# A softmax kernel in a hardware loop of three chunks: each load issued as two transfers of 32 KB per partition instead of one of 64 KB

## The chip, the cores and the metric

One core of one Trainium2 chip. The metric is the device time of one execution in microseconds (us); several executions are timed and their median is quoted. Ratios are the mean time of one kernel's fast runs over that of the other's of the same rounds, so they are not quite the ratio of the medians quoted beside them.

## The reference

A softmax over the last axis of a float32 tensor of 16 x 256 x 32768, with a temperature of 1.0.

```python
def reference(logits, temperature):
    scaled = logits / temperature
    scaled = scaled - scaled.max(axis=-1, keepdims=True)
    exp_scaled = np.exp(scaled)
    return (exp_scaled / exp_scaled.sum(axis=-1, keepdims=True)).astype(np.float32)
```

537 MB are read and 537 MB written, each once.

## The kernel before

Each of the 4096 rows is cut in two, which makes 64 chunks of 128 partitions x 16384 numbers (64 KB per partition, 8.39 MB). A chunk stays in one of three buffers: it is loaded, reduced and exponentiated in four pieces on VectorE and ScalarE, the two halves of a row are combined, the chunk is scaled in place and stored. All transfers are issued by the sync engine, into one queue.

```python
    def step(i: int, turn=None, per_turn: int = 0) -> None:
        g, c = divmod(i, C)
        end = turn is None and g == G - 1
        store(i, _END_DMA if end else CW, turn, per_turn)
        j = i + _BUFS - 1
        if i and j < n_chunks:
            end = turn is None and j // C == G - 1
            load(j, _END_DMA if end else CW, turn, per_turn)
        if c == C - 1 and g + 1 < G:
            ...    # cut: normalise the next chunk

    per_turn = 3
    first = per_turn
    turns = (n_chunks - (_BUFS - 1) - C - first) // per_turn     # 19
    ...    # cut: the first loads, the first chunk
        for i in range(first):
            step(i)
        with tc.For_i(0, turns, 1, iteration_sync="reg_based") as turn:
            for i in range(first, first + per_turn):
                step(i, turn, per_turn)
        for i in range(first + turns * per_turn, n_chunks):
            step(i)
```

Step i stores chunk i and loads chunk i+2 into the buffer that chunk i-1 has left. One turn of the hardware loop has three steps, one for each buffer. The framework puts in all waits: it hands out eight DMA semaphores in turn (counters that a transfer raises when it has landed, and that instructions wait for), and it starts anew with the first of them inside the loop.

Of the kernel before, what the change touches and what calls it, by code (L numbers as in the profile page):

```python
# [9 lines left out]
_CW = 16384  # L10
_BUFS = 3
_PIECE = 4096
_END_DMA = 4096
_END_PIECE = 4096
_DVE_SHARE = 0.625
# [4 lines left out]
def kernel(  # L20
# [19 lines left out]
    CW = min(_CW, W)  # L40
    C = W // CW
# [21 lines left out]
    def spans(total: int, step: int) -> list[tuple[int, int]]:  # L63
        return [(s, min(step, total - s)) for s in range(0, total, step)]

    def rows(i: int, turn, per_turn: int):
        g = i // C
        if turn is None:
            return slice(g * P, (g + 1) * P)
        return bass.ds(turn * (per_turn // C * P) + g * P, P)  # L70

    def load(i: int, step: int, turn=None, per_turn: int = 0) -> None:
        c = i % C
        for s, n in spans(CW, step):
            nc.sync.dma_start(
                out=buf[i % _BUFS][:, s : s + n],
                in_=x[rows(i, turn, per_turn), c * CW + s : c * CW + s + n],
            )

    def store(i: int, step: int, turn=None, per_turn: int = 0) -> None:  # L80
        c = i % C
        for s, n in spans(CW, step):
            nc.sync.dma_start(  # L83
                out=o[rows(i, turn, per_turn), c * CW + s : c * CW + s + n],
                in_=buf[i % _BUFS][:, s : s + n],
            )
# [70 lines left out]
# [4 lines that stand above are left out]
        j = i + _BUFS - 1  # L161
        if i and j < n_chunks:
            end = turn is None and j // C == G - 1
            load(j, _END_DMA if end else CW, turn, per_turn)
        if c == C - 1 and g + 1 < G:
            end = turn is None and g + 1 == G - 1
            normalise(g + 1, _END_PIECE if end else _PIECE)

    per_turn = 3
# [3 lines left out]

    with tc.manual_schedule():
        for i in range(_BUFS):
            load(i, _END_DMA if i < C else CW)
        normalise(0, _PIECE)
        for i in range(first):
            step(i)
# [5 lines that stand above are left out]
# [35 lines left out]
```

## Time and profile before

| | before |
|---|---|
| timed with the changed kernel | 2498.11 us median (2490.05 to 2508.91, 4 runs) |
| profiled span | 2489.5 us |
| DMA queue busy | 99.9% of the span, 431 GB/s |
| VectorE, ScalarE busy | 63%, 55% |

One more view: the waits of the sync engine, which issues all transfers. The columns are: who waited on which line for what, the total in us, how often, and the longest.

```profile
SPq L83 <- DVE x L150: 2102.8, 66, 40.2
SPq L83 <- DMA x<-in_logits_dram: 168.1, 19, 9.5
```

Line 83 is the store. It waits for the engines to finish a chunk. 19 times, once a turn, it also waits for a load, at most 9.5 us; that is a wait which is passed on the way, with the one for VectorE behind it.

### The profile page before, as it was taken

The numbers are of one execution on the slowest core, as the hardware profiler recorded it, in microseconds if no ns is written. First come the engines' busy times: TensorE is split into PE (matmuls) and PEld (weight loads), VectorE is DVE, ScalarE is ACT, GpSimd is POOL, SyncE is SP. The second block draws the span as 40 slices with busy tenths as digits, with TensorE's granted clock in tenths as the row PEclk, the third lists the DMA queues.
The fourth block names the chain that finished last, engine by engine and source line by source line (L and its number), as shares of the span: only waits on it lengthen the run. The fifth ranks groups of instructions, "written<-read, shape, count | busy, mean of one in ns | idle before, by whom it ended". The sixth has DMA issues, their size and how long they took to land. (4 is left out here: it accounts for less than half of the span.)

```text
span 2489.5 us, 4388 instructions
## 1 busy us (share of the span) xinstructions
DVE 1579.6 (63%) x1216; ACT 1368.7 (55%) x833; POOL 0.2 (0%) x4
## 2 busy tenths in 40 slices
DVE  6575665766657666576566665766657666576565
ACT  5464554646546455464554655646546455464555
POOL 0000000000000000000000000000000000000000
DMA  9999999999999999999999999999999999999999
GB/s 421 421 438 433 426 433 435 425 437 437 431 433 435 435 433 436 432 435 432 438 431 436 433 436 437 430 436 433 437 428 437 433 438 429 436 433 432 426 405 404
DMA packets 19733, 1073.79 MB, mean 431 GB/s; under 512 B 2192, under 2 KB 2192, under 8 KB 2192
## 3 DMA queue, kind: packets, MB, share of 16 engines
q1 hardware_dynamic: 19728, 1073.75, 99.9%
q14 instruction: 5, 0.04, 0.0%
HBM read 536.87 MB, written 536.87 MB: 431 GB/s over the span
## 5 line engine op out<-in xcount | busy, mean ns | idle before, releaser
L115 DVE TENSOR_REDUCE nm<-x 128x1 f32<-128x4096 f32 x256 | 1113.7, 4412 | 646.6 <-DMA x<-in_logits_dram 635.9
L122 ACT ACTIVATE x<-x,nm 128x4096 f32<-128x4096 f32 x256 | 949.2, 3708 | 1017.3 <-DVE nm L115 1002.2
L153 ACT ACTIVATE x<-x,f 128x1536 f32<-128x1536 f32 x256 | 382.3, 1564 | 73.5 <-DVE f L147 73.5
L150 DVE TENSOR_SCALAR x<-x,f 128x2560 f32<-128x2560 f32 x256 | 380.2, 1548 | 2.3
L135 DVE CUSTOM_DVE_ANT_0 ttj<-ee,ssum 128x4 f32<-128x4 f32 x64 | 10.4, 163 | 222.5 <-ACT ee L132 222.5
L122 ACT ACTIVATION_READ_ACCUMULATOR x<-x,nm 128x1 f32 x256 | 47.7, 186 | 0.0
L132 ACT ACTIVATE ee<-nm,nMh 128x4 f32<-128x4 f32 x64 | 18.0, 282 | 0.0
L147 DVE TENSOR_SCALAR f<-ee,rS 128x4 f32<-128x4 f32 x64 | 14.7, 229 | 2.2
L146 DVE RECIPROCAL rS<-Sh 128x1 f32<-128x1 f32 x64 | 10.5, 164 | 2.2
L94 DVE TENSOR_TENSOR nMh<-nMh 128x1 f32<-128x1 f32 x64 | 10.2, 159 | 2.2
L94 DVE TENSOR_TENSOR Sh<-Sh 128x1 f32<-128x1 f32 x64 | 10.2, 159 | 2.2
L130 DVE TENSOR_REDUCE nMh<-nm 128x1 f32<-128x4 f32 x64 | 10.0, 157 | 2.2
L91 DVE STREAM_SHUFFLE Sh<-Sh 128x1 f32<-128x1 f32 x64 | 9.7, 152 | 0.0
L91 DVE STREAM_SHUFFLE nMh<-nMh 128x1 f32<-128x1 f32 x64 | 9.7, 151 | 0.0
L122 ACT ACT_TABLE_LOAD x1 | 1.3, 1283 | 8.1 <-DMA x<-in_logits_dram 8.1
L135 DVE DVE_READ_ACCUMULATOR2_ANT Sh<- 128x1 f32 x64 | 5.3, 82 | 0.0
L91 DVE LOAD_MASK_SELECT nMh<-nMh x64 | 0.9, 14 | 2.8
L91 DVE LOAD_MASK_SELECT Sh<-Sh x64 | 0.9, 14 | 2.8
L201 POOL MEMSET const-bfloat16-1.0<- 128x1 bf16 x1 | 0.1, 103 | 0.0
L201 POOL MEMSET const-uint8-127<- 128x1 uint8 x1 | 0.1, 102 | 0.0
L201 POOL MEMSET const-float32-0.0<- 128x1 f32 x1 | 0.1, 99 | 0.2 <-issue 0.2
L201 POOL MEMSET const-float32-1.0<- 128x1 f32 x1 | 0.1, 99 | 0.0
## 6 DMA issues: line engine op xcount, KB each, us to landing
x<-in_logits_dram SPq DMA_DIRECT2D x8, 2048.0 KB, 29.3
out_dram<-x SPq DMA_DIRECT2D x4, 2048.0 KB, 15.9
out_dram<-x SPq DMA_DIRECT2D x63, 29.3
x<-in_logits_dram SPq DMA_DIRECT2D x62, 48.0
```

Source lines behind the costliest of these rows:

```text
L91: nc.vector.stream_shuffle(out=v[:, j + 1 : j + 2], in_=v[:, j : j + 1], mask=mask)
L94: nc.vector.tensor_tensor(out=v[:, j + 1 : j + 2], in0=v[:, j : j + 1], in1=v[:, j + 1 : j + 2], op=op,)
L115: nc.vector.tensor_reduce(out=nm[:, k : k + 1], in_=xc, axis=X, op=A.max, negate=True)
L122: nc.scalar.activation(out=xc, in_=xc, func=Exp, bias=nm[:, k : k + 1], scale=inv_t, accum_out=ssum[:, k : k + 1],)
L130: nc.vector.tensor_reduce(out=nMh[:, 0:1], in_=nm, axis=X, op=A.min)
L132: nc.scalar.activation(out=ee, in_=nm, func=Exp, bias=nMh[:, n_rounds : n_rounds + 1], scale=-1.0)
L135: nc.vector.tensor_tensor_reduce(out=ttj, in0=ee, in1=ssum, scale=1.0, scalar=0.0, op0=A.mult, op1=A.add, accum_out=Sh[:, 0:1],)
L146: nc.vector.reciprocal(out=rS, in_=Sh[:, n_rounds : n_rounds + 1])
L147: nc.vector.tensor_scalar_mul(out=f, in0=ee, scalar1=rS)
L150: nc.vector.tensor_scalar_mul(out=xc[:, :cut], in0=xc[:, :cut], scalar1=f[:, k : k + 1])
L153: nc.scalar.activation(out=xc[:, cut:], in_=xc[:, cut:], func=Copy, scale=f[:, k : k + 1])
L201: nc = _bacc.Bacc("TRN2", target_bir_lowering=False, num_devices=1)
```

## The change

The intent: when a chunk's load comes in two halves, VectorE can start on the first half while the second is on its way, so that the store is ready earlier. The end of the kernel, with transfers of 16 KB per partition, stays as it is.

```diff
+_LOAD = 8192
...
-            load(j, _END_DMA if end else CW, turn, per_turn)
+            load(j, _END_DMA if end else _LOAD, turn, per_turn)
...
-            load(i, _END_DMA if i < C else CW)
+            load(i, _END_DMA if i < C else _LOAD)
```

The program that is built from it differs where the diff doesn't show it. These are the waits of the first store in the loop, before and after (abridged, with the growth of the awaited count in brackets; semaphores named `own` are those of the loop):

```
before: DMACopy out_0_dram<-x0_58 [waits DMAHW0_own (16 more each turn), DVE_own, DMAHW2_own, Activation_own, DMAHW3_own, DMAHW4_own, ...]
after:  DMACopy out_0_dram<-x0_58 [waits DMAHW0_own (32 more each turn), DVE_own, DMAHW3_own, Activation_own, DMAHW4_own, DMAHW5_own, DMAHW6_own, ...]
```

## The prediction

> **What bounds the kernel now.** I read the page first (busy shares, slices, queues), then the sync engine's timeline in the middle and at the loop's end, then times to landing, and last the built program's waits.
>
> ```profile
> DVE 1579.6 (63%) x1216; ACT 1368.7 (55%) x833; POOL 0.2 (0%) x4
> DMA  9999999999999999999999999999999999999999
> q1 hardware_dynamic: 19728, 1073.75, 99.9%
> HBM read 536.87 MB, written 536.87 MB: 431 GB/s over the span
> ```
>
> The engines are a third idle or more; the one DMA queue is busy for 99.9% of the 2489.5 us span. In the DMA view of 200 to 2200 us it moves 434 GB/s, so a transfer of 128 rows of 64 KB (8.39 MB) takes 8.39/434 = 19.3 us, and a chunk (one load, one store) 38.7. 64 chunks at 38.7 are 2477 us: nearly the whole span. A steady chunk in the timeline:
>
> ```profile
> 1042.79 0.34 SPq L83 DMA_DIRECT2D out_dram<-x  x1
> 1043.34 0.35 SPq L75 DMA_DIRECT2D x<-in_logits_dram  x1
> 1052.98 17.40 DVE L115 TENSOR_REDUCE nm<-x 128x1 f32<-128x4096 f32 x4 [10.32 <-DMA x<-in_logits_dram]
> 1075.49 5.94 DVE L150 TENSOR_SCALAR x<-x,f 128x2560 f32<-128x2560 f32 x4
> 1075.55 5.97 ACT L153 ACTIVATE x<-x,f 128x1536 f32<-128x1536 f32 x4 [1.15 <-DVE f L147]
> 1081.78 0.34 SPq L83 DMA_DIRECT2D out_dram<-x  x1
> ...
> out_dram<-x SPq DMA_DIRECT2D x63, 29.3
> x<-in_logits_dram SPq DMA_DIRECT2D x62, 48.0
> ```
>
> A store lands 29.3 us after its issue, though it needs only 19.3: at issue some 10 us of the next chunk's load are still ahead of it. VectorE's wait (10.32) is for that same load. So each store enters the queue 10 us before it would run dry, and the queue never does. It does run dry once, where the hardware loop ends, because the sync engine there waits for every transfer of the loop:
>
> ```profile
> 2319.10 0.35 SPq L75 DMA_DIRECT2D x<-in_logits_dram  x1
> 2367.91 0.34 SPq L83 DMA_DIRECT2D out_dram<-x  x1
> 2368.30 0.42 SPq L75 DMA_DIRECT2D x<-in_logits_dram  x1
> ...
> DMA to landing us min/median/max: 48.1/48.1/48.1
> ...
> DMA to landing us min/median/max: 42.4/42.4/42.4
> ```
>
> The two landing lines belong to the two loads shown. The first lands at 2319.10 + 48.1 = 2367.2, only then is the store issued (2367.91), and the load behind it lands at 2368.30 + 42.4 = 2410.7. Between the two landings lie one store and one load, 38.7 us of work, but 43.5 pass. **One drain of the queue costs 4.8 us**, of which 0.7 is the barrier between 2367.2 and 2367.91. This is the number that my prediction rests on.
>
> **What the Trainium skill says.** Four places of its page "DMA: Bandwidth & Descriptors". "Where 436 GB/s comes from" gives 435 GB/s as the ceiling of the core's 16 DMA engines; the trace agrees with 434 in the steady part, so a faster steady state isn't to be had. "Queues, rings and completion order" says each engine takes descriptors in ring order, which agrees with the landings: 48.0 for a load is 10 of the load before, 19.3 of the store, 19.3 of its own. "Anatomy of one DMA" gives about 2 us of fixed cost (for the GpSimd path), mostly completion[...]. Here the first load's 2 MB (4.8 us at 434 GB/s) are issued at 0.74 and VectorE starts on them at 8.10: 2.5 us. "Why a DMA increments its semaphore by 16 and not by 1" says that two DMAs in flight on one semaphore can't be told apart by its count and each slot should have its own. No trace of before shows it, but the compiler of this kernel must respect it, and there the change hurts.
>
> **The change part by part.**
>
> *Added transfers.* 62 loads become 124: 62 x 128 = 7,936 more data packets, 62 x 16 = 992 more small ones. From the DMA view: 200 to 2200 us (64 KB packets alone) has 14,881 packets, 1,648 of them small, at 100.2%: 1.002 x 16 x 2000 / 13,233 = 2.423 us per packet. 2472 to 2484 us (16 KB packets) has 367, 48 small, at 101.7%: 1.017 x 16 x 12 / 319 = 0.612. Four of those are 2.448, so three more packets cost 25 ns, 8 each. Each engine gets 62 x 8 = 496 more: about 4 us, with completions **5 us**. Issuing costs the sync engine 62 x 0.35 us, beside a full queue: nothing.
>
> *Earlier start.* The first half of a chunk lands 9.7 us before the second, so VectorE does two of four reductions (2 x 4.35 = 8.7 us) earlier and the store is ready 8.7 us earlier. With a full queue this makes the queue longer, 18.7 us for 10, and nothing faster. At the end of the kernel too: the last loads and stores follow one another in the queue, and the stretch from 2396 to 2489 is 98% busy.
>
> *A new wait.* The program has eight DMA semaphores, handed out in turn, and inside the loop the counting starts anew. Before, a turn has six transfers (store, load, three times), each with its own semaphore. Now it has nine: store, load a, load b, three times; the ninth, load b of the third step, gets the first semaphore, that of the turn's first store. In the built program this first store waits for that semaphore to reach 32 more per turn (16 before), that is for **both** transfers of the turn before on it, and the second is the transfer issued immediately ahead of this store. So the store, the first of every turn, can't enter the queue until the queue is empty. The data doesn't need it: that load goes to another buffer. The order of instructions alone doesn't show it; the list of waits does.
>
> How often: (64 - 2 - 1 - 3) // 3 = 19 turns; the first has no turn before it, so **18 drains**; the one at loop exit is there already. Is the wait really last? Yes: the store's chunk is finished some 18 us before that load lands (the longer queue), and even on the old schedule 10 us before. After a drain the turn's other stores are issued with 18 us or more queued, and nothing else runs dry: the second store also needs the first landed, at about 22 us, while the load behind the first runs till 41.
>
> Cost of one: 4.8 as above, less the barrier's 0.7, plus about 0.2 to get from the landing to the issue: 4.3 us. It contains completion, issue, first data, and a slowdown when all engines restart together (the load after the restart took 2410.7 - (2367.91 + 21.7) = 21.1 us after its store landed, 21.7 being that store's own time to landing, where 19.3 is usual). A turn has four more transfers after those two; at the kernel's start, likewise from rest, such transfers lose some tenths each, so I take **4.7**. 18 x 4.7 = 85 us, with 5 for packets **+90 us**: the profiled span becomes about 2580. The three timed runs of before average 2502, so 2502 + 90 = 2592; I shade it to **2588**, because 4.7 rests on one drain.
>
> **The rivals.**
> 1. *Saturated, nothing happens* (no drain, only packets): 2505 + 5 = 2510. For it: 99.9% busy. Against it: the wait's count, which is in the program.
> 2. *The earlier start pays at the end.* The chain that ended last goes through the load that lands at 2410.7 and then VectorE; 8.7 us less there would give 2496. Against it: the queue is busy behind that chain until the end.
> 3. *Drains are cheap*: only landing to issue and issue to data, 2 us, because the restart slowdown at the loop's end was chance. 18 x 2 + 5 = 41: 2543, within 2%.
> 4. *Half rows read worse from HBM.* The 16 KB windows show 1% per byte for the smaller pieces; twice that on half of the bytes were 25 us on top of the drains.
>
> **Range and chances.** Low end: 2.6 us a drain, 47 + 5 on 2496 (between the fastest run and the mean): 2548. High end: 5.9 a drain, 106 + 5 on 2509: 2620. 2% of 2505 is 50 us, so 2.5 us a drain passes it; rivals 1 and 3 together get 0.12. Faster needs more than the 435 ceiling has: 0.01. Slower: 0.87.
>
> **What would show it right or wrong.** In the changed profile: 18 stores, 116.3 + 4.7 = 121 us apart, issued right after the landing of a load with VectorE long idle, and a sync wait on a load that ends them; queue share near 97%, mean rate near 1073.8/2580 = 416 GB/s; 28,661 packets (19,733 + 7,936 + 992); stores landing at a median of about 38 us (29.3 + 8.7), those right after a drain at 22; VectorE's busy time unchanged. If the page still shows 431 GB/s and no such gaps, rival 1 is right and I misread the wait. If the gaps are there but 2 us each, rival 3. A rate below 428 GB/s between drains would be rival 4.

## The result

The changed kernel takes 2567.07 us (median of 4, 2565.23 to 2568.25), the kernel before 2498.11. The ratio is 1.0273 with a 95% interval of 1.0224 to 1.0322: slower. The time lies within the predicted range, 21 us under its point.

The page of the changed kernel: span, queue, totals, and the transfers with their median time from issue to landing.

```profile
span 2563.4 us, 4789 instructions
...
DVE 1585.3 (62%) x1216; ACT 1368.7 (53%) x833; POOL 0.2 (0%) x4
...
DMA  9999999999999999999999999999999999999999
...
DMA packets 28660, 1073.79 MB, mean 419 GB/s; under 512 B 3184, under 2 KB 3184, under 8 KB 3184
...
q1 hardware_dynamic: 28656, 1073.75, 98.4%
...
x<-in_logits_dram SPq DMA_DIRECT2D x124, 4096.0 KB, 47.4
...
out_dram<-x SPq DMA_DIRECT2D x63, 38.3
```

The bytes and the engines' work are those of before; the rate has fallen from 431 to 419 GB/s, and the queue is no longer busy all the time. The "9" in all 40 slices doesn't show that, since a slice of 64 us hides a gap of 3. A store now takes 38.3 us to land where it took 29.3: the queue ahead of it is 9 us longer. So the earlier start works as intended. It just doesn't help.

One turn of the loop in the timeline of the changed kernel (start, duration, engine, line; the last bracket is idle time before it, and what ended it):

```profile
973.72 5.94 DVE L151 TENSOR_SCALAR x<-x,f 128x2560 f32<-128x2560 f32 x4
...
998.60 8.75 DVE L116 TENSOR_REDUCE nm<-x 128x1 f32<-128x4096 f32 x2 [0.96 <-DMA x<-in_logits_dram]
998.87 0.36 SPq L84 DMA_DIRECT2D out_dram<-x  x1
999.50 1.58 SPq L76 DMA_DIRECT2D x<-in_logits_dram  x2
...
1020.84 0.36 SPq L84 DMA_DIRECT2D out_dram<-x  x1
1021.41 0.88 SPq L76 DMA_DIRECT2D x<-in_logits_dram  x2
...
1061.14 0.36 SPq L84 DMA_DIRECT2D out_dram<-x  x1
1061.81 0.90 SPq L76 DMA_DIRECT2D x<-in_logits_dram  x2
...
1119.08 0.35 SPq L84 DMA_DIRECT2D out_dram<-x  x1
```

VectorE's part of the chunk is scaled at 973.72 + 5.94 = 979.7. Its store is issued at 998.87, 19.2 us later, and 0.3 us after VectorE was woken by another chunk's load (998.60). From this store to the next of its kind, at 1119.08, a turn takes 120.2 us; before, it took 116.0, three chunks of 38.66 (from the load issued at 1004.92 to that at 2280.63 are 33 chunks, 1275.7 us). And in the waits of the sync engine:

```profile
SPq L84 <- DMA x<-in_logits_dram: 1351.9, 38, 55.6
SPq L84 <- DVE x L151: 892.8, 48, 37.1
```

The store's waits for a load have risen from 168.1 us (at most 9.5) to 1351.9 (at most 55.6), and from 19 to 38 times. They are of two kinds: from 998 to 1062 us, about half a turn, the same view has two, 74.2 us together, the longer of 55.6. The shorter one, before the turn's third store, is passed on the way as before. The long one, before the first, is new, and it ends last. It happens 18 times: the drained stores are issued from 277.11 to 2321.61 us, 120.3 us apart on average, each about 0.4 us after the landing.

**Where one drain's time goes**, from the times to landing of these same transfers (a drain: the queue runs empty before the next transfer is issued). In order: the two halves of the load ahead, the store, the first and the second half behind it, the turn's last two halves.

```profile
DMA to landing us min/median/max: 47.3/51.9/56.4
...
DMA to landing us min/median/max: 21.8/21.8/21.8
...
DMA to landing us min/median/max: 30.9/30.9/30.9
...
DMA to landing us min/median/max: 41.1/41.1/41.1
...
DMA to landing us min/median/max: 47.2/51.7/56.3
```

The load issued second at about 942.1 lands 56.4 us later, at 998.5. The store issued at 998.87 lands after 21.8, at 1020.7: 22.2 us after the load, where one transfer takes 19.3 in a full queue, so 2.9 are lost. The two halves behind it land at 999.5 + 30.9 and 1000.1 + 41.1 = 1041.2: 20.5 us for the pair where 19.4 are usual, 1.1 lost. From there to the landing of the last load of the turn (issued at 1062.4, 56.3 to landing, so 1118.7) 77.5 us pass for four transfers of 19.3 or 19.4: nothing lost. Together 4.0 us in this turn.

### The profile page after: what moved, and what is told of

It reads as the page before. It is cut to its first block, busy times and chain, and to the rows that moved or that the text cites. A ratio compares the mean times of both kernels' runs of the same rounds, so it can differ in the third digit from the quotient of the medians.

```text
span 2563.4 us, 4789 instructions
## 1 busy us (share of the span) xinstructions
DVE 1585.3 (62%) x1216; ACT 1368.7 (53%) x833; POOL 0.2 (0%) x4
## 3 DMA queue, kind: packets, MB, share of 16 engines
q1 hardware_dynamic: 28656, 1073.75, 98.4%
## 5 line engine op out<-in xcount | busy, mean ns | idle before, releaser
L136 DVE CUSTOM_DVE_ANT_0 ttj<-ee,ssum 128x4 f32<-128x4 f32 x64 | 10.4, 162 | 222.5 <-ACT ee L133 222.5
## 6 DMA issues: line engine op xcount, KB each, us to landing
out_dram<-x SPq DMA_DIRECT2D x63, 38.3
```

What stands on the lines that cost most here:

```text
L136: nc.vector.tensor_tensor_reduce(out=ttj, in0=ee, in1=ssum, scale=1.0, scalar=0.0, op0=A.mult, op1=A.add, accum_out=Sh[:, 0:1],)
```

## The experiments

The theory: nine transfers a turn, eight semaphores, so the first store of a turn waits for the transfer issued just ahead of it and the queue runs dry once a turn. The main rival: halved loads are slow in themselves (more packets, a worse order of reads, upset timing). All results were correct. The first four ran on one chip beside before at 2491.77 us (8 runs), the next four beside before at 2501.49 (7 runs).

### 1. Eight transfers a turn

```diff
-            load(j, _END_DMA if end else _LOAD, turn, per_turn)
+            load(j, _END_DMA if end else (CW if j % _BUFS == 1 else _LOAD), turn, per_turn)
```
(and the same where the first buffers are loaded)

> Two of the three loads of a turn in halves, the third (buffer x1) whole: eight transfers a turn, so no two of a turn share a semaphore. Theory (the ninth transfer's shared semaphore drains the queue once a turn): no drain, about +3 us for packets over before, so 2500 to 2510, ratio 1.00; no store issued only after a load landed with VectorE long done. Rival (halves of loads are slow in themselves: more packets, worse order of HBM reads, or upset timing by the earlier start): two thirds of the change's 69 us, about 2545. Nearly the same number of transfers as the changed kernel, so the two are 40 us apart.

Measured: 2496.53 us (2495.77 to 2496.81), ratio 1.0019 (1.0002 to 1.0036). From first store to first store in its timeline:

```profile
1004.98 0.35 SPq L84 DMA_DIRECT2D out_dram<-x  x1
...
1121.06 0.36 SPq L84 DMA_DIRECT2D out_dram<-x  x1
```

116.1 us, as before. Two thirds of the loads are halved and the loss is gone. The rival would have had 2545. The time is some 3 us under the band that I wrote, because before's own median beside it was lower (2491.77); the ratio is as expected.

### 2. Nine transfers a turn with whole loads

```diff
+    junk = [pool.tile([P, 128], fp32, tag=f"j{b}", name=f"j{b}") for b in range(_BUFS)]
...
+    def extra(i: int, turn=None, per_turn: int = 0) -> None:
+        nc.sync.dma_start(out=junk[i % _BUFS], in_=x[rows(i, turn, per_turn), 0:128])
...
             load(j, _END_DMA if end else CW, turn, per_turn)
+            if turn is not None:
+                extra(j, turn, per_turn)
```

> The kernel before, loads whole, plus one transfer of 64 KB (512 B a row, into a spare tile nobody reads) behind each load of the loop: nine transfers a turn, the ninth sharing the first store's semaphore. Theory: the drain is back without any halved load; 18 drains of about 3.9 us and some 5 us for the small transfers: 2565 to 2580, ratio 1.03. Rival (halves are what is slow): 57 small transfers of 64 KB, 3.7 MB or 9 us at the steady rate, more likely less than 15: 2505 to 2515.

Measured: 2584.52 us (2582.79 to 2585.2), ratio 1.0369 (1.0352 to 1.0387). Its waits:

```profile
SPq L84 <- DMA j<-in_logits_dram: 864.0, 18, 49.1
```

No load is halved, and the loss is back and larger. A store waits exactly 18 times for a spare transfer whose data it has no use for. The time is 4.5 us above the band that I wrote: the 57 small transfers cost more than I allowed or the drain behind them is longer; I didn't take that apart.

### 3. A tenth transfer added to the changed kernel

```diff
         store(i, _END_DMA if end else CW, turn, per_turn)
+        if turn is not None and i % _BUFS == 1:
+            extra(i, turn, per_turn)
```
(`junk` and `extra` as in 2)

> The changed kernel plus one transfer of 64 KB a turn, in the middle step: ten transfers a turn. Now the first store shares its semaphore with the last step's first half load (and only the next load with its second half), so it is issued with half a load, about 9.7 us, still queued. Theory: more transfers than the changed kernel, but no drain: 2500 to 2515, ratio 1.00. Rival (packets, halves): above the changed kernel, 2570.

Measured: 2505.26 us (2504.72 to 2506.24), ratio 1.0055 (1.0038 to 1.0072). **More work, and some 62 us less than the changed kernel** (by the ratios to before, 1.0055 against 1.0273, 54). In its timeline the waits of the shared semaphores can be seen, and that they are harmless here:

```profile
1084.46 0.36 SPq L85 DMA_DIRECT2D out_dram<-x  x1
1093.88 0.92 SPq L77 DMA_DIRECT2D x<-in_logits_dram  x2
```

The store goes in when the first half of the load ahead of it has landed. The next load waits 9.4 us more, for the second half; by then the store is queued, and the queue stays full.

### 4. Six chunks in a turn

```diff
-    per_turn = 3
-    first = per_turn
+    per_turn = 6
+    first = 3
```

> The changed kernel with six chunks in a turn for three: every load still in halves, eighteen transfers a turn, the same data transfers in all. The first store of a turn again shares with the last step's first half load, not with the second. Theory: no drain between turns, 2500 to 2512 (2498 plus 5 for packets and a few us for a longer tail outside the loop), ratio 1.00. Rival (halves are slow): 2567 as the changed kernel. A variant of the theory in which each turn boundary itself costs would give half the loss, 2535.

Measured: 2501.70 us (2501.0 to 2502.56), ratio 1.0038 (1.0022 to 1.0055). Every load is halved and the data transfers are those of the changed kernel. What differs is how many transfers one turn of the loop has, and with it which of them share a semaphore.

```profile
q1 hardware_dynamic: 28656, 1073.75, 99.7%
```

Since both move the same packets, the two pages show what a drain consists of. 99.7% of 2500.7 us leaves 7.5 us in which an average DMA engine has no packet, and 98.4% of 2563.4 leaves 41. So 33 of the 63 us between the two spans are an idle queue. The rest is packets that take longer: by the traces one of 64 KB takes 2.451 us on average in the changed kernel and 2.422 here, one of 32 KB 1.237 and 1.221. They are longest just after a restart: 64 KB packets that start 10 to 20 us after a drained store take 2.61 us, those from 40 us on 2.42.

### 5. Loads in quarters

```diff
-_LOAD = 8192
+_LOAD = 4096
```

> The changed kernel with each load in four transfers of 16 KB a row: fifteen transfers a turn, four packets for one. By the list of waits the first store now shares its semaphore with a quarter of the middle step's load, long landed, so there is no drain. Theory: only packets, 62 x 3 more transfers at the 8 x 8 ns + completion of the prediction, some 0.08 us each, or 15 us: ratio to before about 1.006. Rival (splitting loads is what costs): twice to three times the change's loss, 2640 or more, since there are three more transfers a load for one.

Measured: 2507.13 us (2506.64 to 2507.89), ratio 1.0031 (0.9976 to 1.0086); before varied much in these rounds, so I compare profiled spans as well: 2505.6 against 2489.5, 16 us for 186 more transfers, 0.09 us each, against the 0.08 expected. The interval excludes the rival, which had 2640. Cutting loads into more pieces is cheap, and in four pieces 60 us cheaper than in two, because fifteen transfers share their semaphores differently from nine.

### 6 and 7. No hardware loop

```diff
-        with tc.For_i(0, turns, 1, iteration_sync="reg_based") as turn:
-            for i in range(first, first + per_turn):
-                step(i, turn, per_turn)
-        for i in range(first + turns * per_turn, n_chunks):
+        for i in range(first, n_chunks):
             step(i)
```

Number 6 is the changed kernel with this edit, number 7 the kernel before with it.

> The changed kernel without the hardware loop: all steps written out, loads in halves. Each transfer then waits for the one eight before it on its semaphore, which has landed. Theory: no drain at turns and none at the loop's end (4 us): packets +5, drain -4, so level with before, ratio 0.998 to 1.003. Rival (halves): 2567. Unknown: whether fetching a program of some 4,000 instructions instead of a loop costs something; the trace would show it as a DMA queue of instructions or as gaps.

> The kernel before without the hardware loop. Theory: its one drain, at the loop's end, goes: 4 to 5 us less than before, ratio 0.998, and the queue never empties after its start. If the drain at the loop's end is no real cost, level with before.

Measured: halves 2496.01 us (2495.64 to 2496.59), ratio 0.9987 (0.9933 to 1.0042); whole 2503.13 (2500.47 to 2505.96), ratio 1.0019 (0.9963 to 1.0074). The first is as expected: no loop, no shared counts, no loss. **The second is a miss**: the drain at the loop's end is gone, and yet no gain can be seen. The interval still includes the expected 0.998, but all four runs are slower than before's faster ones beside them (2490.68 to 2491.65), and the profiled span is 9.2 us longer than before's. The end of its trace (stretch, its length, VectorE, ScalarE, GpSimd busy, clock, DMA share, GB/s), and the same place in number 6:

```profile
2450.00:2460.00 10.00, 10.00 (x3) 7.14 (x3) 0.00 (x0) 1.00 1.02 434
2460.00:2470.00 10.00, 6.30 (x12) 8.26 (x7) 0.00 (x0) 1.00 0.83 361
2470.00:2480.00 10.00, 6.26 (x6) 5.97 (x4) 0.00 (x0) 1.00 0.82 345
...
2460.00:2470.00 10.00, 6.82 (x11) 8.38 (x7) 0.00 (x0) 1.00 0.59 251
```

The share falls to 0.82 although the last stores aren't through. I read this as some of the 16 DMA engines having finished their rows and others not: in the trace the 16 completions of the last loads lie 8.4 us apart from first to last. The engines drift apart while the queue is full. In before they are 3.6 us apart ahead of the drain at the loop's end and at most 1.5 after it, so that drain lines them up again.

That doesn't explain the miss, though. In number 6 the engines drift further, to 12.0 us, and the share falls lower, to 0.59; yet its span is 4.8 us shorter than that of number 7 (2493.9 for 2498.7). What goes with the longer span is the time of single packets: one of 64 KB takes 2.432 us on average in number 7 and 2.425 in before, which over 1,000 such packets per engine is 7 of the 9.2 us. Runs 9 and 10 find the same in before itself; why it is so stays open.

### 8. Stores in two

```diff
-        store(i, _END_DMA if end else CW, turn, per_turn)
+        store(i, _END_DMA if end else CW // 2, turn, per_turn)
```
(in the kernel before, whose loads are whole)

> The kernel before with the stores of all steps but the last chunk's in two halves, loads whole: nine transfers a turn, the ninth is again the load ahead of the first store. And inside the loop a store waits for the store before it to land (the list of waits has it), so that every second half waits for its first half with nothing queued behind it. Theory: four drains a turn for one: 18 + 3 x 19 = 75 drains at 3 to 4 us, 225 to 300 us on before, 2715 to 2790, if a drain costs the same wherever it lies. If a drain costs only once per turn, or the cost lies in halving itself, about 2570.

Measured: 2714.24 us (2713.55 to 2715.35), ratio 1.086 (1.0801 to 1.0919), just under the band. Its waits:

```profile
SPq L83 <- DMA out_dram<-x: 1222.6, 57, 27.6
...
SPq L83 <- DMA x<-in_logits_dram: 538.9, 18, 30.1
```

57 + 18 = 75 waits that end last on a transfer, as counted beforehand. The profiled span is 2712.4, which is 222.9 over before; less 5 for the 63 more transfers, 218 / 75 = 2.9 us each. So the loss grows with the number of drains, and these, most of them with a store after a store, are cheaper on average than the 4.0 of the changed kernel.

### 9 and 10. The kernel before, twice more

The executions of before fall into two groups, near 2491 and from 2501 to 2512, all of the same clock; those of the changed kernel lie within 3 us. Both runs are the unchanged program.

> The kernel before, unchanged, for one more profile: its timed runs of the same state lie in two groups, near 2491 and 2501 to 2512, while those of the changed kernel lie within 3 us. If this profile falls in the slower group it shows where 10 to 20 us go. Theory: some engines fall behind the others (their completions of one load spread over more than 4 us) because single packets take longer, with the queue never empty. Rival: the queue runs dry at some turns, since only 10 us are queued when a store is issued. If it falls in the faster group again, the question stays open.

> As the run before it, a second attempt to catch an execution of the slower group in a profile. Same theories, same numbers.

Measured: 2507.96 us and 2491.35 us, single runs of state unknown. So one profile of each group. Of the slower one (run 9), the queue, and a stretch of 250 us in its middle:

```profile
q1 hardware_dynamic: 19728, 1073.75, 99.7%
...
1750.00:2000.00 250.00, 154.33 (x116) 130.01 (x79) 0.00 (x0) 1.00 1.00 428
```

The same stretch in the faster profile of before:

```profile
1750.00:2000.00 250.00, 164.48 (x122) 141.79 (x85) 0.00 (x0) 1.00 1.00 433
```

The queue is just as full (1.00, 99.7%), and its rate is 1% lower here (over nine such stretches from 0 to 2250 us, 431 for 433 GB/s). So the rival written there, a queue that runs dry, falls. Single packets take longer: by the trace the mean packet of 64 KB takes 2.437 us for 2.425, over 1,000 per engine 12 of the 16.6 us between the spans. The engines are further apart too, 8.6 us between the first and last completion of a load late in the loop, for 3.6 in the faster profile. But the distance alone costs little: run 10, of the faster group, has 5.7 us with the same span of 2489.5 and packets of 2.424 us, and number 6 has 12.0 without being slow. In the changed kernel, which lines its engines up every turn, it is 1.1 us at most from 500 us on. Why packets are stretched in one execution and not in another stays open.

**A version that beats both?** Number 6 has the best median beside its own neighbours (2496.01 for 2501.49), but its interval includes 1, and it isn't better than before's faster group. At 434 GB/s of the ceiling of 435 that the prediction cites there is hardly anything left to win in the steady part.

## Why the prediction was right, and where its size was off

**What bounds the kernel.** Right. The queue was full and the engines idle; making the store ready earlier made the queue longer (38.3 us to landing; predicted about 38) and nothing faster. 1, 3, 4 and 6 agree: halved loads without a drain run level with before, within 0.6%.

**Added packets.** Right in size: 8,927 more packets by the page (8,928 predicted), about 5 us. Number 5, with three times as many added transfers, had 16 us for the expected 15.

**The new wait.** Right, and the cause is shown from both sides. With the count of transfers at eight, ten or eighteen a turn the loss is gone though loads stay halved (1, 3, 4); with nine it is there with whole loads (2). The number of drains is right too: 18 in the changed kernel, 18 counted by name in 2, and 18 + 57 in 8.

**Cost of one drain.** This is the term that was mis-sized: 4.7 us, measured 4.0 in the turn taken apart above; the whole span gives (2563.4 - 2489.5 - 5) / 18 = 3.8. For the first store I had 2.6 (the 22.4 us from the load's landing at 2367.2 to its own, less 19.3, less 0.7 for the barrier, plus 0.2), and it is 2.9. I had 1.8 for the slow load behind it, and it is 1.1. I had 0.4 for the rest of the turn, and it is nothing. I had a sample of one, at the loop's end, and it was a bad one for the second part. 18 x 0.8 (4.7 less 3.9, the middle of 4.0 and 3.8) are 14 of the 21 us.

**The base.** The other 7: I added the 90 us to 2502, the mean of three runs two of which were of the slower group, and shaded by 4 (the rivals are reckoned partly from 2505, which fits neither). But that group's extra 10 to 20 us don't add to the drains: none of the changed kernel's four runs shows a second group. From 2490.5, the mean of before's two faster runs, the sum would have been 2580, less 14 for the drains 2566, for 2567 measured. Why the changed kernel has no slower group isn't shown. That its drains line the engines up isn't needed for it: 5 and 6 have no drain in each turn and engines 10.4 and 12.0 us apart, and yet their four runs each lie within 1.3 us, in rounds in which before was in its slower group four times of seven. Number 7, whole loads without drains, spreads over 5.5 us.

**The rivals.** 1 (nothing happens) and 2 (gain at the end) fell with the result. 3 (2 us a drain) was too low. 4 (half rows read worse) fell with 1, 4 and 6. Of the signs that I listed, the queue's share was 98.4% for the "near 97%" predicted, the rate 419 GB/s for 416. The rate follows from the smaller drain. The share doesn't alone: 97% counts a drain as idle queue throughout, and by the comparison in 4 only about half of it is.

## What to carry to other kernels

In a loop, count the transfers of one turn against the number of DMA semaphores, and read the list of waits of the first one: if it shares a semaphore with the transfer issued just ahead of it, the queue runs dry once a turn, as here, whatever the data needs. Here one transfer more or less in a turn, or six steps for three, mended it; the new list of waits tells whether it has. When the queue is full, getting stores ready earlier wins nothing, so here such a change had only risks; and a page that shows "9" in every slice can hide a gap of some us in each turn, which the issue times show at once.

## What the Trainium skill lacked or had wrong

- "DMA: Bandwidth & Descriptors", section "Why a DMA increments its semaphore by 16 and not by 1", advises one semaphore for each slot in flight. It doesn't say what a program pays that must reuse one in a loop: a full wait for the newest transfer on it, here 18 drains and 69 us (2498.11 to 2567.07).
- The same page's "Anatomy of one DMA" gives about 2 us of fixed cost for the GpSimd path. For the sync engine's queue under load it has no figure for running dry and restarting. Here, in the turn taken apart, it is 2.9 us for the store that restarts it and 1.1 for the load behind; 2.9 on average where mostly a store follows a store (run 8).
- "DMA: Bandwidth & Descriptors" says in its section on iDMA, within an explanation that it marks as unconfirmed, that a bulk load runs at the pace of its slowest engine. It has nothing on how far the 16 engines drift apart under a queue that is always full: 3.6, 5.7 and 8.6 us apart in three profiles of before, with 2489.5, 2489.5 and 2506.1 us of span, and 12.0 in run 6 with 2493.9.
- "Where 436 GB/s comes from" on that page: the ceiling of 435 GB/s held, with 434 in the steady part, reads and writes together. The same section says that for transfers between HBM and SBUF the HBM side, about 358 GB/s, is what binds; that did not hold in this program, which runs on one core and moves all its 434 GB/s between the two.
